# A two-block transformer on one core: chunks regrouped in the feed-forward, two norms' squares moved from GpSimd, operand steps made one block earlier

## The chip, the core and the metric

The kernel runs on one core of a Trainium2 chip. Five engines work there from queues of their own: TensorE (PE in the profile; PEld is its weight load), VectorE (DVE), ScalarE (ACT), GpSimd (POOL) and SyncE (SP, which only issues transfers here; POOL issues some too). An engine takes its instructions strictly in the order of its queue, and waits at the head of the queue for what the instruction needs. The metric is the time of one launch in device microseconds (us).

## The reference

Two transformer blocks on 512 tokens of 1024 features, in float32. The first has two layers; each mixes tokens (a short convolution in the first layer, attention in a window in the second, and attention to 256 memory rows in both) and ends in a feed-forward. The second block is sparse attention with retention beside it; its first norm follows directly on the first block's last norm. What the change touches is this, cut from the reference:

```
def rmsnorm(x, g):
    x32 = x.astype(jnp.float32)
    y = x32 * lax.rsqrt(jnp.mean(x32 * x32, axis=-1, keepdims=True) + EPS)
    return (y * g.astype(jnp.float32)).astype(x.dtype)
...
        x = x + jnp.concatenate([y_tok, y_mem], axis=-1) @ w_out
        h = rmsnorm(x, norm_ffn[i])
        x = x + (jax.nn.silu(h @ w_gate[i]) * (h @ w_up[i])) @ w_down[i]
    return rmsnorm(x, final_norm)
```

The feed-forward is 2816 wide.

## The kernel before, in words

The activations lie with features on the partitions: `self.x` is eight chunks of 128 features by 512 tokens. Every float32 product is made of three TensorE matmuls: each operand is split into a high part (ScalarE copies it, L70) and a low part (VectorE subtracts, L76 or L80), and high by high, low by high and high by low are added in PSUM (L120 to L122, or L575 to L577). Weights come through `weights`: a transfer on SP's queue into one of two raw buffers `wr`, then `wh` by ScalarE and `wl` by VectorE, three buffers each. A raw buffer is free for the next transfer when its last reader is done.

`ffn` runs over 22 chunks of 128 of the feed-forward's width, in the groups of `FFG`. Chunks 0 to 4 are plain (`plain_gate_up`: 48 matmuls of 512 columns). From chunk 5 on, gate and up together are seven smaller products (`gate_up`: 84 matmuls of 256 columns), with sums of weights (`pair_weights`: `s1` to `s4` by VectorE at L555, then split) and sums of activations. The latter, called B here, are made once a feed-forward by the generator `halves`, two chunks of x at a step, so four steps. While a group's chunks are computed, the down projection of the group before it is done between them: eight outputs `down`, one for each chunk of x, of 3 matmuls of 512 columns for each chunk in the group. VectorE subtracts each output from x (L638). `share` says how many of the eight come in which chunk. The last group's eight follow when all chunks are done; in the first layer's feed-forward the projections of the memory rows (`mem_kv`) stand ahead of them.

After the last group x is complete, and the next layer's norm needs the sum of its squares over features. `square_sum` adds the squares of the eight chunks to `acc` (after the second feed-forward also to `acc2`, weighted by a gain). With `first` false GpSimd squares chunks 0 to 6 (L157) and adds chunks 1 to 6 (L166); ScalarE squares chunk 7 (L159) and VectorE adds it. With `first` true ScalarE squares all eight and VectorE adds. `token_mean` sums `acc` over partitions with tiny matmuls (L174), `rsqrt` works on 4 columns, and `spread` makes from it a row over all partitions (L203, L206), called `Rb` in the second layer and `R` in the second block. The next projections use x without the norm's factor (`gained`: `gh` and `gl`, or `g`), and the factor is put on their results; they need `R` only when they are done.

The Python code is not the order in the queues: a scheduler in the compiler puts each engine's instructions into an order of its own, which is then fixed.

Of the kernel before, what the change touches and what calls it, by code (L numbers as in the profile page):

```python
# [21 lines left out]
NEG = -1.0e30  # L22
WMAX = 1152
KWORDS = 2 * 9 * 64
FFG = [(0, 4), (4, 8), (8, 12), (12, 16), (16, 19), (19, 22)]
PLAIN = 5


class Build:
# [590 lines left out]
    def ffn(self, layer, between_last=None):  # L620
        nc, T = self.nc, self.T
        gain = self.gain(2 + layer)
        h = self.gained(self.x, gain)
        R = B = act = None

        def down(i, act, g):

            f0, f1 = FFG[g]
            n = f1 - f0
            w = []  # L630

            def one(c):
                if not w:
                    w.extend(self.weights(T["w_down"][layer, i][:, f0 * 256:f1 * 256], 2 * n, 128))
                ps = self.psum("po" if (2 * i + c) % 3 == 2 else "tp")
                self.proj(ps, None, act, [t[:, c * n:c * n + n] for t in w])
                x = self.x[2 * i + c]
                nc.vector.tensor_tensor(x, x, ps, op=ALU.subtract)  # L638

            return [lambda: one(0), lambda: one(1)]  # L640

        for g, (f0, f1) in enumerate(FFG):
            last = act
            todo = [] if last is None else [p for i in range(4) for p in down(i, last, g - 1)]
            act = []
            n = f1 - f0
            shares = [0] * n if last is None else [4, 2, 1, 1] if f0 < PLAIN else [8 * (i + 1) // n - 8 * i // n for i in range(n)]
            for f, share in zip(range(f0, f1), shares):
                mine, todo = todo[:share], todo[share:]

                def between(i):
                    for p in mine[i * (len(mine) // 2):] if i else mine[:len(mine) // 2]:
                        p()

                if f < PLAIN:
                    a, R = self.plain_gate_up(layer, f, h, R)
                    if f == 0:
                        steps = self.halves(self.x, R, gain)
                    else:
                        sets = next(steps)  # L660
                    between(0)
                    between(1)
                else:
                    if f == PLAIN:
                        B = [[s[i] for s in sets] for i in range(7)]
                    a = self.gate_up(T["w_gu"][layer, f - PLAIN], B, between)
                act.append(a)
        if between_last:
            between_last()
        for i in range(4):  # L670
            for p in down(i, act, len(FFG) - 1):
                p()

    def layer_b(self):
        nc, T = self.nc, self.T
        hk = self.gained(self.x, self.gain(4), ["pa"] * 3 + ["pb"] * 5)
        rs, R = self.norm_row(1e-5, "Rb")
        rs = self.keep(rs, "rsb")
        h = self.gained(self.x, self.gain(1))
        xd = self.dr.tile([8, 128, 512], F32, name="xres")  # L680
        for c in range(8):
            nc.gpsimd.dma_start(xd[c], self.x[c])
        ks = []
        for b in range(2):
            ps = self.psum("pp")
            self.proj(ps, T["w_kv_k"][b], hk)
            kk = self.slot("t", name="k")
            self.mul(kk, ps, R)
            ks += self.stack_k(kk, tag="x")
        vs = []  # L690

        def done(tb, ps):
            v = self.value_tile()
            self.fill_values(v, ps, rs[:, tb:tb + 1])
            vs.append(v)
            if tb == 3:
                vs.append(self.last_value(ps, rs[:, 3:]))

        self.proj_tok(T["w_kv_v"], hk, 256, 4, done, tag=("pp", "lg"))
        mk, mv = self.mem1  # L700
        qs = []
        for b in range(2):
            qs += self.stack_q(self.queries(T["b_w_q"][6 + b], h, R))
        ym = self.mem_attention(qs, mk, mv)
        ys = []
        for pair in range(6):
            q = self.stack_q(self.queries(T["b_w_q"][pair], h, R))
            bias = self.bias(pair)
            po = self.psum("po")
            nc.tensor.matmul(po.rearrange("p (a b) -> p a b", a=4), self.zero, self.zero.unsqueeze(1).to_broadcast([128, 4, 128]), start=True, stop=False)  # L710
            for odd in range(2):
                self.band_head(po, 2 * pair + odd, odd, q[odd], ks, vs, bias[:, odd])
            ys.append(self.split(po, "b", name="y"))
        self.x = [self.slot("x", name="x") for _ in range(8)]
        for c in range(8):
            nc.sync.dma_start(self.x[c], xd[c])
        self.residual(T["b_w_out"], ys + ym, [6, 7, 0, 1, 2, 3, 4, 5])
# [209 lines left out]
    def second(self):  # L927
# [4 lines left out]
        g2 = self.const("g2", [128, 8])  # L932
        self.mul(g2, gf, gf)
        h = self.gained(self.x, gg)
        a1, a2 = self.square_sum(self.x, gain2=g2)
        m1 = self.token_mean(a1, 512, 1e-5, 1024.0)
        m2 = self.token_mean(a2, 512, 0.0, 1024.0)
        t = self.small(4, name="m3")
# [1 line left out]
        rs = self.keep(self.rsqrt(t), "rs12")  # L940
        R = self.spread(rs, "R2")
# [235 lines left out]
def _feat(w):  # L1177

    k, c = w.shape
    return np.ascontiguousarray(w.reshape(k // 128, 128, c // 128, 128).transpose(2, 1, 0, 3)).reshape(c // 128, 128, k)  # L1180
# [48 lines left out]
def _pack(i):  # L1229
# [18 lines left out]
    down = np.stack([_feat(m) for m in w["w_down"]]).reshape(2, 4, 2, 128, 22, 128).transpose(0, 1, 3, 2, 4, 5)  # L1248
    a["w_down"] = np.concatenate([down[:, :, :, :, f0:f1].reshape(2, 4, 128, -1) for f0, f1 in FFG], 3)
    a["w_kv_k"] = _feat(w["w_kv"][:, :256])  # L1250
# [46 lines left out]
```

## Time and profile before

| | before |
|---|---|
| median of 3 runs (lowest, highest) | 1681.77 us (1681.52, 1689.32) |
| profiled execution: time, span | 1686.65 us, 1684.9 us |
| mean granted TensorE clock | 0.987 of 2.4 GHz |
| PE busy | 1619.6 us, 96% |
| VectorE, ScalarE, GpSimd busy | 1248.2, 756.6, 196.4 us |

The span runs from the first to the last instruction; the launch's time is 1.75 us more. All times below are counted from the start of the span. In rows of the timeline, what stands in brackets is the idle time of the engine ahead of the instruction and what ended it.

### The profile page before, as it was taken

Reading aid. Unit: us, or ns where it says so; the run is one execution under the profiler, and the core shown is the slowest. Engines: PE = TensorE matmul, PEld = TensorE weight load, DVE = VectorE, ACT = ScalarE, POOL = GpSimd, SP = SyncE. Lnnn points to the kernel's source line nnn. Section 1 sums busy time; section 2 is a strip of 40 time slices with the busy share of each in tenths; the row PEclk is TensorE's granted clock in tenths of the full one; section 3 lists DMA queues with packets and bytes.
Section 4 is the critical chain, followed back from the end, with each engine's and each line's share of the span. In section 5 each row is a group of like instructions: output and inputs, shape, how many; then the busy total and the mean of one; then the engine's idle time right before and its main releaser. Section 6 shows DMA issues by size and latency. Waiting matters only on the chain.

```text
span 1684.9 us, 24388 instructions
## 1 busy us (share of the span) xinstructions
PE 1619.6 (96%) x9408; PEld 1415.5 (84%) x9408; DVE 1248.2 (74%) x2330; ACT 756.6 (45%) x1404; POOL 196.4 (12%) x186
## 2 busy tenths in 40 slices
PE   8999999999999699999999999979999999999997
PEld 6887888999999588888889999857788888888887
DVE  7866788787776869877877777579788977764443
ACT  6532244454445467634444444324556533333233
POOL 1112410000000600041000000151001000010010
PEclk9999999999999799999999999989999999999999
DMA  6222222332234522232233233332511122243342
GB/s 199 88 88 88 100 76 100 101 113 101 101 104 123 183 94 77 68 101 88 85 103 113 89 113 98 91 118 86 172 45 57 40 76 92 70 150 113 124 158 88
DMA packets 51572, 171.60 MB, mean 102 GB/s; under 512 B 6680, under 2 KB 6880, under 8 KB 51328
## 3 DMA queue, kind: packets, MB, share of 16 engines
q1 hardware_dynamic: 45504, 151.11, 27.1%
q0 software_dynamic: 5376, 18.82, 3.3%
q8 instruction: 74, 1.21, 0.3%
q14 instruction: 42, 0.34, 0.1%
q10 hardware_dynamic: 576, 0.11, 0.0%
HBM read 160.56 MB, written 11.81 MB: 102 GB/s over the span
## 4 chain that ended last, share of the span: by engine, by line
PE 71%; DVE 15%; DMA 7%; ACT 3%; issue 3%; POOL 1%; SPq 0%; DVEq 0%; ACTq 0%; POOLq 0%
PE pp L122 8%; PE pp L121 8%; PE pp L120 8%; PE lg L120 4%; PE lg L121 4%; PE lg L122 4%; DMA wr<-in_w_gu_dram 3%; DVE wl L80 3%; PE pp L575 3%; PE pp L576 2%; PE pp L577 2%; PE tp L262 2%; PE tp L120 2%; PE tp L121 2%; PE tp L122 2%
## 5 line engine op out<-in xcount | busy, mean ns | idle before, releaser
L70 ACT ACTIVATE wh<-wr 128x1024 fp32r<-128x1024 f32 (+3 forms) x246 | 251.9, 1025 | 371.7 <-PE pp L121 129.1
L80 DVE TENSOR_TENSOR wl<-wr,wh 128x1024 fp32r<-128x1024 f32 (+3 forms) x246 | 305.6, 1243 | 70.1 <-ACT wh L70 68.8
L122 PE MATMUL pp<-g,wl 128*128 128x512 f32 x592 | 235.0, 397 | 11.2 <-DVE wl L80 11.2
L120 PE MATMUL pp<-g,wh 128*128 128x512 f32 x592 | 235.8, 399 | 8.1 <-ACT wh L70 8.1
L121 PE MATMUL pp<-g,wh 128*128 128x512 f32 x592 | 234.1, 396 | 0.2 <-DVE g L76 0.2
L122 PEld LDWEIGHTS pp<-g,wl 128*128 128x128 f32 x592 | 112.2, 189 | 33.7 <-DVE wl L80 13.0
L120 PEld LDWEIGHTS pp<-g,wh 128*128 128x128 f32 x592 | 112.6, 190 | 30.3 <-ACT wh L70 8.9
L121 PEld LDWEIGHTS pp<-g,wh 128*128 128x128 f32 x592 | 112.4, 190 | 21.6 <-DVE g L76 0.9
L70 ACT ACTIVATE s<-s 128x512 fp32r<-128x512 f32 x136 | 85.0, 631 | 62.5 <-DVE s L555 59.7
L120 PE MATMUL tp<-acth,wh 128*128 128x512 f32 x264 | 104.4, 396 | 5.7 <-DVE x L638 3.3
L121 PE MATMUL tp<-actl,wh 128*128 128x512 f32 x264 | 104.0, 394 | 0.0
L122 PE MATMUL tp<-acth,wl 128*128 128x512 f32 x264 | 103.4, 392 | 0.0
L80 DVE TENSOR_TENSOR s<-s,s 128x512 fp32r<-128x512 f32 x136 | 90.3, 685 | 1.9 <-ACT s L70 1.7
L575 PE MATMUL pp<-Bh,s 128*128 128x256 f32 x272 | 77.5, 285 | 3.4 <-ACT g L70 3.4
L575 PE MATMUL lg<-Bh,s 128*128 128x256 f32 x272 | 77.8, 286 | 1.3 <-DVE u L582 1.3
L577 PE MATMUL pp<-Bh,s 128*128 128x256 f32 x272 | 77.4, 285 | 0.3
L577 PE MATMUL lg<-Bh,s 128*128 128x256 f32 x272 | 77.4, 285 | 0.0
L555 DVE TENSOR_TENSOR s<-wr,wr 128x512 f32<-128x512 f32 x68 | 46.8, 688 | 39.7 <-DMA wr<-in_w_gu_dram 39.7
L120 PEld LDWEIGHTS tp<-acth,wh 128*128 128x128 f32 x264 | 50.0, 190 | 16.4 <-ACT wh L70 2.6
L122 PEld LDWEIGHTS tp<-acth,wl 128*128 128x128 f32 x264 | 50.0, 190 | 10.6
L638 DVE TENSOR_TENSOR x<-x,tp 128x512 f32<-128x512 f32 x72 | 49.2, 683 | 12.6 <-PE tp L122 12.6
L576 PE MATMUL lg<-Bl,s 128*128 128x256 f32 x204 | 58.1, 285 | 0.0
(503 smaller groups left out, 4557.5 us busy)
## 6 DMA issues: line engine op xcount, KB each, us to landing
wr<-in_w_gu_dram SPq DMA_DIRECT2D x68, 512.0 KB, 3.8
wr<-in_w_in_dram SPq DMA_DIRECT2D x44, 512.0 KB, 3.5
wr<-in_w_down_dram SPq DMA_DIRECT2D x32, 512.0 KB, 3.7
wr<-in_a_w_in_dram SPq DMA_DIRECT2D x18, 512.0 KB, 3.5
wr<-in_w_down_dram SPq DMA_DIRECT2D x16, 384.0 KB, 3.3
wr<-in_w_gate_dram SPq DMA_DIRECT2D x10, 512.0 KB, 3.5
wr<-in_w_up_dram SPq DMA_DIRECT2D x10, 512.0 KB, 3.4
wr<-in_a_w_out_dram SPq DMA_DIRECT2D x8, 512.0 KB, 3.4
```

Of the source, the lines that this page charges most:

```text
L70: self.nc.scalar.activation(out, in_, AF.Copy, scale=scale)
L80: self.nc.vector.tensor_tensor(out, x, hi.bitcast(F32), op=ALU.subtract)
L120: mm(ps, ah, bh, start=start, stop=False)
L121: mm(ps, ah, bl, start=False, stop=False)
L122: mm(ps, al, bh, start=False, stop=stop)
L262: self.nc.tensor.transpose(ps[:, c:c + 128], src, self.ident)
L555: nc.vector.tensor_tensor(t, a, b, op=ALU.add)
L575: mm(ps, ah, bh, start=start and j == 0, stop=False, skip_group_check=not start)
L576: mm(ps, ah, bl, start=False, stop=False, skip_group_check=not start)
L577: mm(ps, al, bh, start=False, stop=j == 3, skip_group_check=not start)
L638: nc.vector.tensor_tensor(x, x, ps, op=ALU.subtract)
```

## The change

Three edits. The groups of chunks become 4, 4, 3, 4, 3, 4 in place of 4, 4, 4, 4, 3, 3, so the last down projection has four chunks and is 96 matmuls in place of 72; the total is the same, and the weights of `w_down` are packed to suit. The step of `halves` for x's first two chunks comes in chunk 0 instead of chunk 1, and so on: all four steps are done after chunk 3 instead of chunk 4. The two norms that follow a feed-forward (in `layer_b`, and at the start of `second`) take their squares from ScalarE and their sums from VectorE; the norm inside each layer, ahead of the feed-forward, stays as it was.

```
-FFG = [(0, 4), (4, 8), (8, 12), (12, 16), (16, 19), (19, 22)]
+FFG = [(0, 4), (4, 8), (8, 11), (11, 15), (15, 18), (18, 22)]
...
                     if f == 0:
                         steps = self.halves(self.x, R, gain)
-                    else:
-                        sets = next(steps)
+                    sets = next(steps, None) or sets
...
-        rs, R = self.norm_row(1e-5, "Rb")
+        rs, R = self.norm_row(1e-5, "Rb", True)
...
-        a1, a2 = self.square_sum(self.x, gain2=g2)
+        a1, a2 = self.square_sum(self.x, first=True, gain2=g2)
```

What this makes of the queues is seen at three places. The first is VectorE's queue at the end of the first feed-forward, from the last chunk of x (`x_88`) to the first split of a weight of the next layer (`wl_5583`, the first projection's). `acc` is the sum of squares, `m` and `ri` are the norm's small columns. Before:

```order
L638 TENSOR_TENSOR x_88<-x_88,tp_5445 128x512
L76 SCALAR_TENSOR_TENSOR g_5562<-x_86,gains,g_5562 128x512
L76 SCALAR_TENSOR_TENSOR g_5565<-x_87,gains,g_5565 128x512
L76 SCALAR_TENSOR_TENSOR gl_5485<-x_88,gains,gh_5484 128x512
L166 TENSOR_TENSOR acc_5488<-acc_5488,sq_5508 128x512
L76 SCALAR_TENSOR_TENSOR g_5568<-x_88,gains,g_5568 128x512
L176 TENSOR_SCALAR m_5516<-tp_5511 128x4
L80 TENSOR_TENSOR wl_5583<-wr_5581,wh_5582 128x1024
```

And now:

```order
L638 TENSOR_TENSOR x_88<-x_88,tp_5442 128x512
L166 TENSOR_TENSOR acc_5488<-acc_5488,sq_5505 128x512
L76 SCALAR_TENSOR_TENSOR g_5559<-x_85,gains,g_5559 128x512
L76 SCALAR_TENSOR_TENSOR gl_5485<-x_88,gains,gh_5484 128x512
L166 TENSOR_TENSOR acc_5488<-acc_5488,sq_5508 128x512
L76 SCALAR_TENSOR_TENSOR g_5562<-x_86,gains,g_5562 128x512
L176 TENSOR_SCALAR m_5516<-tp_5511 128x4
L76 SCALAR_TENSOR_TENSOR g_5565<-x_87,gains,g_5565 128x512
L183 TENSOR_SCALAR ri_5518<-m_5516 128x4
L76 SCALAR_TENSOR_TENSOR g_5568<-x_88,gains,g_5568 128x512
L184 TENSOR_SCALAR ri_5518<-ri_5518 128x4
L80 TENSOR_TENSOR wl_5583<-wr_5581,wh_5582 128x1024
```

Six more additions to `acc` stand in this queue ahead of the last (one is in the piece), and between `m` and the weight's split stand two more `g`. In TensorE's queue the place is the same before and after: four matmuls of the next layer, the tiny matmuls on `acc_5488`, then the first matmul that needs `wl_5583`.

The second place is TensorE's queue at the end of the second feed-forward, where the first projection of the second block (`pp_11094`) follows on the last down projection. Before, every row of the first matmuls up to the tiny ones on the two sums:

```order
L120 MATMUL pp_11094<-g_10954,wh_11096 128x512
L121 MATMUL pp_11094<-g_10954,wh_11096 128x512
L120 MATMUL pp_11134<-g_10954,wh_11136 128x512
L121 MATMUL pp_11134<-g_10954,wh_11136 128x512
L122 MATMUL pp_11094<-g_10954,wl_11097 128x512
...
L174 MATMUL tp_11010<-ones,acc_10978 128x2 x4
L174 MATMUL tp_11017<-ones,acc_2007_10979 128x2 x4
```

And now (eighteen matmuls of `pp_11094` are left out, in regular order):

```order
L120 MATMUL pp_11094<-g_10954,wh_11096 128x512
L121 MATMUL pp_11094<-g_10954,wh_11096 128x512
L122 MATMUL pp_11094<-g_10954,wl_11097 128x512
...
L174 MATMUL tp_11010<-ones,acc_10978 128x2 x4
L174 MATMUL tp_11017<-ones,acc_2007_10979 128x2 x4
L120 MATMUL pp_11094<-g_10975,wh_11096 128x512
```

The tiny matmuls, which wait for the sums, stood behind 13 matmuls and now stand behind 21. The split `wl_11097` stood in VectorE's queue behind the last chunk of x; it now stands behind the fourth:

```order
L638 TENSOR_TENSOR x_7098<-x_7098,tp_10868 128x512
L166 TENSOR_TENSOR acc_10978<-acc_10978,sq_10986 128x512
L80 TENSOR_TENSOR wl_11097<-wr_11095,wh_11096 128x1024
L638 TENSOR_TENSOR x_7099<-x_7099,tp_10888 128x512
L76 SCALAR_TENSOR_TENSOR g_10963<-x_7098,gg,g_10963 128x512
```

The third place is VectorE's queue in chunk 4, ahead of the first `gate_up` (chunk 5), whose raw weights are `wr_2264` and `wr_2265`. Before, the fourth step of `halves` (`Bh`, `t`) and three chunks of x stood between `u_2168` and the last reader of `wr_2264`, which is `s_461`:

```order
L80 TENSOR_TENSOR Bh_2190<-m_437_2177,Bh_2190 128x512
L638 TENSOR_TENSOR x_81<-x_81,tp_2202 128x512
L80 TENSOR_TENSOR Bh_2193<-t_438_2178,Bh_2193 128x512
L638 TENSOR_TENSOR x_82<-x_82,tp_2216 128x512
L80 TENSOR_TENSOR wl_2269<-wr_2264,wh_2268 128x1024
```

And now no step of `halves` stands there:

```order
L76 SCALAR_TENSOR_TENSOR u_2189<-lg_2158,Rf_345_1769 128x512
L80 TENSOR_TENSOR wl_2269<-wr_2264,wh_2268 128x1024
L80 TENSOR_TENSOR actl_2193<-u_2189,acth_2192 128x512
L80 TENSOR_TENSOR a_456_2272<-wr_2265,a_456_2272 128x512
L638 TENSOR_TENSOR x_81<-x_81,tp_2202 128x512
L555 TENSOR_TENSOR s_457_2275<-wr_2265,wr_2264 128x512
L555 TENSOR_TENSOR s_459_2280<-s_457_2275,wr_2264 128x512
L555 TENSOR_TENSOR s_461_2285<-wr_2264,wr_2265 128x512
```

The readers of `wr_2264` moved up; the fourth step's 11 instructions are one chunk earlier. Between the two feed-forwards, and behind the first projections of the second block, the queues of TensorE, VectorE and ScalarE are the same but for the order of some 40 rows of VectorE.

## Rows read from the trace of the kernel before

**Rows 1.** Busy us by stage: stretch, length, PE, PEld, DVE, ACT, POOL, PEclk, DMA share, GB/s.
```profile
262.00:350.00 88.00, 85.13 (x595) 78.83 (x594) 70.33 (x115) 41.95 (x70) 0.00 (x0) 1.00 0.31 102
815.00:895.00 80.00, 75.66 (x517) 70.14 (x516) 61.64 (x101) 36.25 (x61) 0.00 (x0) 0.98 0.30 94
350.00:500.00 150.00, 150.00 (x1028) 139.85 (x1027) 111.61 (x182) 68.81 (x113) 0.00 (x0) 1.00 0.31 103
560.00:592.00 32.00, 19.66 (x72) 15.29 (x71) 26.67 (x41) 11.07 (x16) 20.66 (x21) 0.73 0.49 166
1100.00:1137.00 37.00, 25.44 (x100) 19.77 (x100) 29.49 (x58) 9.48 (x12) 18.19 (x19) 0.82 0.32 111
```

**Rows 2.** Timeline of TensorE, end of the first feed-forward: start, duration, engine, line.
```profile
566.89 0.39 PE L120 MATMUL pp<-gh,wh 128*128 128x512 f32 x1
...
579.19 1.87 PE L174 MATMUL tp<-ones,acc 128*128 128x2 f32 x8 [10.94 <-DVE acc L166]
582.44 0.80 PE L122 MATMUL pp<-gh,wl 128*128 128x512 f32 x1 [1.38 <-DVE wl L80]
...
588.15 0.40 PE L120 MATMUL pp<-gh,wh 128*128 128x512 f32 x1
```

**Rows 3.** VectorE's groups by shape, 556 to 579: count, busy us, mean ns.
```profile
L76 DVE SCALAR_TENSOR_TENSOR g<-x,gains,g 128x512 fp32r<-128x512 f32 x7 | 9.6, 1385 | 0.0
L76 DVE SCALAR_TENSOR_TENSOR gl<-x,gains,gh 128x512 fp32r<-128x512 f32 x7 | 8.8, 1263 | 0.0
L638 DVE TENSOR_TENSOR x<-x,tp 128x512 f32<-128x512 f32 x5 | 3.4, 675 | 0.0
```

**Rows 4.** Busy us in two more stretches, columns as in the first group.
```profile
556.00:579.00 23.00, 12.24 (x53) 9.50 (x51) 22.92 (x23) 12.10 (x18) 22.08 (x21) 0.83 0.48 170
1150.00:1170.00 20.00, 17.63 (x116) 16.23 (x115) 19.60 (x36) 11.47 (x20) 1.66 (x1) 1.00 0.16 53
```

**Rows 5.** Timelines of VectorE, GpSimd and ScalarE, end of the first feed-forward.
```profile
571.24 2.91 DVE L76 SCALAR_TENSOR_TENSOR g<-x,gains,g 128x512 fp32r<-128x512 f32 x1
575.32 3.21 POOL L682 DMA_DIRECT2D xres<-x  x6
577.21 0.61 ACT L159 ACTIVATE sq<-x 128x512 f32<-128x512 f32 x1
577.80 0.74 DVE L76 SCALAR_TENSOR_TENSOR gl<-x,gains,gh 128x512 fp32r<-128x512 f32 x1
578.46 0.68 DVE L166 TENSOR_TENSOR acc<-acc,sq 128x512 f32<-128x512 f32 x1
```

**Rows 6.** Timeline of TensorE, end of the second feed-forward.
```profile
1096.18 0.39 PE L120 MATMUL po<-acth,wh 128*128 128x512 f32 x1
...
1098.22 0.39 PE L120 MATMUL tp<-acth,wh 128*128 128x512 f32 x1
...
1110.11 0.56 PE L120 MATMUL tp<-acth,wh 128*128 128x512 f32 x1 [2.16 <-DVE x L638]
...
1113.86 0.40 PE L120 MATMUL pp<-g,wh 128*128 128x512 f32 x1
...
1123.17 0.80 PE L122 MATMUL pp<-g,wl 128*128 128x512 f32 x1 [8.24 <-DVE wl L80]
...
1134.36 1.02 PE L206 MATMUL tp<-dg,ones 128*128 128x512 f32 x2
```

**Rows 7.** Timeline of VectorE: the first instruction that uses the row R.
```profile
1136.05 0.69 DVE L73 TENSOR_TENSOR f<-pp,R 128x512 f32<-128x512 f32 x1 [0.50 <-ACT R L70]
```

**Rows 8.** Timeline of TensorE: first matmuls of two blocks of gate_up in sequence.
```profile
296.42 0.28 PE L575 MATMUL pp<-B,wh 128*128 128x256 f32 x1
...
309.69 0.28 PE L575 MATMUL pp<-B,wh 128*128 128x256 f32 x1
```

**Rows 9.** Timeline of VectorE: the last reader of the first gate_up's first raw weights.
```profile
269.05 0.68 DVE L555 TENSOR_TENSOR s<-wr,wr 128x512 f32<-128x512 f32 x1
```

**Rows 10.** Timeline of TensorE: first matmul of the first layer's last down projection.
```profile
549.90 0.47 PE L120 MATMUL po<-acth,wh 128*128 128x512 f32 x1 [0.89 <-DVE s L336]
```

**Rows 11.** Timeline of ScalarE: the split of the first gate_up's first raw weights.
```profile
255.90 1.06 ACT L70 ACTIVATE wh<-wr 128x1024 fp32r<-128x1024 f32 x1 [1.84 <-DMA wr<-in_w_gu_dram]
```

## The prediction, written before the changed kernel had run

> **What bounds the kernel now.** I read the busy time by stage first, because a mean of 96% for TensorE says nothing of where the rest goes. In the middle of a feed-forward TensorE is busy 150.00 of 150.00 us: no change of order can gain there. It idles in four places [rows 1]: 32.00 − 19.66 = 12.34 us at the end of the first feed-forward, 37.00 − 25.44 = 11.56 at the end of the second, and 2.87 and 4.34 in their first `gate_up` blocks. All three edits aim at these, so the sum is made there.
>
> At the first end, the timeline of TensorE shows that it begins the next layer's matmuls at 566.89, does four, and then waits 10.94 for `acc` and 1.38 for a split weight; it resumes at 582.44 [rows 2]. Then it runs at the lower of its two clock levels (1.2 GHz): 13 matmuls take 5.71 us to 588.15, where at the full clock one output of nine takes 1098.22 − 1096.18 = 2.04 us, or 0.227 each [rows 2, 6]. That is 5.71 − 2.95 = 2.8 lost on top.
>
> Why is `acc` late? VectorE is busy 22.92 of the 23.00 us from 556 to 579, and GpSimd 22.08 [rows 4]. VectorE's 14 splits of x there take 1385 and 1263 ns, and one takes 2.91 us; the same split takes 0.74 at 577.80, where GpSimd computes nothing any more [rows 3, 5]. The update of x from PSUM takes its 675 ns throughout. So 14 splits cost 18.4 us instead of 10.4: 8 us of VectorE's queue go to GpSimd's squares and sums, and the last chunk of x, and `acc` behind it, are late by that.
>
> At the second end the same happens earlier: the down projection itself waits for x (11.56 − 8.24 = 3.32 in two waits), runs nine matmuls from 1110.11 to 1113.86 in 3.75 instead of 2.04, and then waits 8.24 for `wl` in VectorE's queue [rows 1, 6].
>
> **The change, part by part.**
>
> *First end.* The 13 instructions of arithmetic on GpSimd are gone; GpSimd only issues transfers. ScalarE gets seven more squares of 0.61, VectorE six more sums of 0.68 [rows 5]. ScalarE was busy 12.10 of 23.00, so 4.3 more fit [rows 4]. On VectorE a chunk of x is now one update, two splits and one sum, 0.68 + 2 × 0.74 + 0.68 = 2.84, some 0.08 less each in sequence, so 2.5; TensorE's output of 12 matmuls takes 2.72. VectorE keeps pace, where before it had 3.2 a chunk against 2.04. Behind the last update come a sum, two splits and the last sum: 0.7 + 0.6 + 0.7 + 0.7 + 0.7 = 3.4, so the wait of 10.94 becomes about 3 (TensorE has four matmuls to do meanwhile). From there to the weight it was 582.44 − 579.19 = 3.25; two splits more stand in that stretch of the queue, + 1.4. Gain: 7.9 − 1.4 = 6.5. The slow stretch behind it stays if the two waits, of 3 each, lower the clock as that of 2.16 did [rows 6]; otherwise 2.8 more.
>
> Ahead of it two things get tighter. The memory rows' projections have 1 output of nine instead of 2 as cover behind the last `gate_up`, 2.0 us less, and the first down matmul now uses the second pair's weights, whose load starts only when a raw buffer of the memory weights is free. TensorE already waits 0.89 at that spot [rows 10]. Bounds: nothing, or 2.0 plus one split by ScalarE of 1.06 [rows 11]. I take 1.5. A gain at the clock of between 0 and 2.8, say 1.5, evens this out. **First end: 6.5, from 3 to 10.**
>
> *Second end.* VectorE's chunk is one update, one split and two sums, again 2.5 to 2.9 against 2.72, so the two waits for x go (3.3 and 1.7 at the low clock). `wl_11097` stands five chunks earlier, so TensorE does not wait for it (8.24), and the tiny matmuls stand behind 21 matmuls, 4.8 us after the last down: the last sums end about 3.6 after it. No wait is left. Without waits TensorE reaches `pp` at 1113.86 − 3.3 − 1.7 = 1108.9; 21 matmuls (4.8), the tiny ones (at most the 1.87 of rows 2, twice as many at double the clock) and 23 matmuls (5.2) lead to L206 at 1120.8 instead of 1134.36 [rows 2, 6]. `f` follows 1.69 later as before, at 1122.4 instead of 1136.05 [rows 6, 7]. I count to `f` because VectorE sets the time after it (19.60 of 20.00 busy [rows 4]), so a lead of TensorE alone would be lost. **14, from 9 to 16**; the lower end is a wait of 5 for the sums, as if a chunk took VectorE 3.3.
>
> *Operand steps.* In chunk 4, the last reader of the first raw buffer ends at 269.73 [rows 9]. Its weights were split by ScalarE from 255.90 to 256.96 [rows 11]; from there the new queue has only a split of 1.2, one of `act`, `a`, x and three sums ahead of the release, 1.2 + 6 × 0.65 = 5.1, so it comes at about 262. The loads behind it start 4 to 8 us earlier, and the waits of the first blocks, 2.87 and 4.34, and 1.6 at the low clock, have that as cover. The steps cost nothing one chunk earlier: each chunk had one, now chunks 0 to 3 have it. **6.5 of 8.8, from 0 to 9.**
>
> *Groups.* Blocks with two outputs of nine matmuls are shorter than any steady one before: 84 × 0.12 + 2 × 2.04 = 14.2 us, eight in each feed-forward. The supply has followed at 309.69 − 296.42 = 13.27 [rows 8], but over two blocks only. Bounds 0 and 16 × 0.5; I take **−1**.
>
> Two rules of the Trainium skill bear on this. Rows 3 and 5 show that splits with two inputs in SBUF stretch and updates with one input in PSUM don't. "SBUF — State Buffer", section "Who interferes with whom", says that a VectorE instruction with two SBUF inputs contends with GpSimd instructions that read SBUF, and that the loser blocks for the whole instruction; the trace's 2.91 for one of 0.74, 2.2 more than alone, needs two GpSimd instructions in its way, not one. By the rule the sums that VectorE takes over have GpSimd no more as a rival, and the total stands. "ScalarE: Activation LUTs", section "What ACT_TABLE_LOAD costs", speaks against the squares: a change of table set costs 2.66 us, and if each square among the copies cost one, 16 would be 43 us. The square at 577.21 stands among copies at 0.61 without one [rows 5]; the sum goes by that.
>
> **Sum.** 6.5 + 14 + 6.5 − 1 = 26. The profiled execution took 1686.65, 4.9 more than the median of 1681.77; its waits are taken as the median's, so 1686.65 − 26 = 1660.7 in its terms and **1655.8** in those of the median.
>
> **Rivals.**
>
> *A: only the ends gain.* The first blocks wait on transfers, whose time doesn't change, and the freed VectorE time is spent waiting for them: operand steps 0. For it: VectorE is busy only 70.33 of 88.00 there [rows 1], so it isn't full. Against: the raw buffer's release at 269.73 is VectorE's. 1681.8 − 19.5 = 1662.3.
>
> *B: the stretched splits are not GpSimd's doing* but the transfers' (170 GB/s in that stretch [rows 4]). Then the splits stay at 1.3, VectorE's chunk is 4.0 us against 2.72, and each end is later by the six or so sums of 0.68: − 4 at each, with + 5.5 left of the rest: 1684. Against: at 577.80, between GpSimd's six issues and with transfers under way, a split took 0.74 [rows 5]. The same skill page ("SBUF: two separate sides") says that engines and transfers don't contend; by it this rival is out.
>
> *C: slower.* The 16 blocks of 14.2 us outrun the supply of weights. If a block's three loads and their splits need more than 14.2 + 26/16 = 15.8 us, the loss eats the gain; at 17, it is 45 − 27 = 18 us: 1700. Against: 13.27 [rows 8], and 15.6 us blocks without any wait [rows 1].
>
> *D: nothing moves*, because what is gained at the ends is waited for behind them, where VectorE is full: 1681. Against: VectorE's queue itself starts 13.7 earlier.
>
> **Chances.** Forecast 0.62, A 0.22, a larger gain (all of the bounds, 1681.8 − 36 = 1646) 0.07, B and D 0.06, C 0.03. The range that leaves out no more than 2 in 10 is 1646 to 1667. What a measurement here can tell from no change is 0.5%, 8.4 us: faster 0.91, same 0.05, slower 0.04.
>
> **What would show it.** Right: at the first end TensorE waits about 3 us for `acc`; every split of x takes 0.75; at the second end no wait over 1 us until `R` is used, and the granted clock stays at 1.00 there; waits under 3 us in all in the first blocks; no new waits in blocks with two outputs. Wrong: splits over 1 us without GpSimd's arithmetic (B), TensorE waiting for `wh` or `g` in chunks 11 to 14 and 18 to 21 (C), or a new wait before the first layer's last down projection of more than 3 us.

## The result, and the profile after

The changed kernel takes 1664.85 us (median of 4 runs, 1661.98 to 1666.17) against 1683.68 for the kernel before in the same runs: a ratio of 0.9884, 95% interval 0.9866 to 0.9903. That is 19.5 us faster. The prediction said 26 us and 1655.8, with a range of 1646 to 1667. The spans of the two profiled executions differ by 1684.9 − 1663.6 = 21.3 us.

The view of busy time by stage of the changed kernel, the stages as in [rows 1] with the second end where it now lies (stretch, length, PE, PEld, DVE, ACT, POOL, PEclk, DMA share, GB/s):

```profile
262.00:350.00 88.00, 85.46 (x583) 79.44 (x583) 64.13 (x104) 38.94 (x66) 0.00 (x0) 0.98 0.34 108
815.00:895.00 80.00, 77.14 (x530) 71.91 (x529) 60.40 (x98) 37.57 (x62) 0.00 (x0) 0.98 0.32 105
560.00:592.00 32.00, 26.53 (x105) 21.27 (x104) 26.40 (x52) 18.16 (x28) 4.85 (x8) 0.84 0.51 177
1080.00:1120.00 40.00, 39.52 (x181) 32.31 (x180) 36.91 (x78) 17.89 (x24) 6.59 (x11) 1.00 0.48 162
```

At the second end TensorE idles 0.48 of 40 us and its clock stays at 1.00; at the first end its idle time went from 12.34 to 5.47. The first blocks, which the operand steps were to clear, idle 2.54 and 2.86 us: in the first feed-forward that is what it was (2.87).

The timeline of TensorE in the changed kernel shows the same places as [rows 2, 6, 10] (start, duration, operation; in brackets the idle time ahead and what ended it):

```profile
265.21 0.28 PE L575 MATMUL pp<-B,wh 128*128 128x256 f32 x1
...
273.26 0.44 PE L575 MATMUL pp<-Bh,s 128*128 128x256 f32 x1 [2.14 <-ACT g L70]
...
528.34 0.40 PE L120 MATMUL tp<-acth,wh 128*128 128x512 f32 x1
...
541.12 0.39 PE L142 MATMUL tp<-wh,gm 128*128 128x256 f32 x1 [2.32 <-ACT wh L70]
547.23 0.50 PE L120 MATMUL po<-acth,wh 128*128 128x512 f32 x1 [0.85 <-ACT wh L70]
...
574.37 1.86 PE L174 MATMUL tp<-ones,acc 128*128 128x2 f32 x8 [2.62 <-DVE acc L166]
579.08 0.79 PE L122 MATMUL pp<-gh,wl 128*128 128x512 f32 x1 [2.85 <-DVE wl L80]
...
1078.01 0.40 PE L120 MATMUL tp<-acth,wh 128*128 128x512 f32 x1
...
1106.61 1.84 PE L174 MATMUL tp<-ones,acc 128*128 128x2 f32 x16
...
1113.65 1.02 PE L206 MATMUL tp<-dg,ones 128*128 128x512 f32 x2
```

The wait of 10.94 for `acc` is 2.62 and that of 1.38 for the weight is 2.85 (the prediction had 3 and 2.8). At the second end the tiny matmuls and L206 wait for nothing. That was close: VectorE's last sum there,

```profile
1105.67 0.68 DVE L166 TENSOR_TENSOR acc<-acc,sq 128x512 f32<-128x512 f32 x1
```

ends 0.26 us before TensorE comes to it at 1106.61. New are the waits at 273.26 and 541.12 and, at the same spot of the second feed-forward,

```profile
823.30 0.58 PE L575 MATMUL pp<-Bh,s 128*128 128x256 f32 x1 [2.24 <-ACT g L70]
```

The granted clock falls at two of them. Busy time by stage of the changed kernel, right behind 273.26 and 823.30:

```profile
273.40:276.80 3.40, 3.40 (x15) 3.20 (x16) 2.97 (x6) 1.67 (x4) 0.00 (x0) 0.51 0.20 24
823.00:826.40 3.40, 3.10 (x13) 3.06 (x14) 3.11 (x6) 1.53 (x4) 0.00 (x0) 0.50 0.00 0
```

Each of these stretches at the lower level (1.2 GHz) costs some 1.7 us, half its length, against the upper one. Before, the first feed-forward's blocks ran at 1.00 throughout (0.98 now in the first stage above), and the second's had one such stretch behind the wait of 1.74 at 884.13.

With these rows the 21.3 us can be placed. The change also moves matmuls from one stretch to the next (behind the last `gate_up` there is one output of nine instead of two, and the last down has 96 matmuls instead of 72), and each is 0.227 us of TensorE. So the first layer's blocks lose 15 matmuls, its memory rows lose 9 and its last down gains 24. In the second layer the last down is counted with the outputs that stand behind the last `gate_up`. The gain of a stretch is its time before, plus the work moved in, minus its time after.

| stretch of TensorE | before | work moved in | after | gain | predicted |
|---|---|---|---|---|---|
| first layer: first `gate_up` to end of the last | 265.80 | −3.4 | 263.13 | −0.7 | +2.75 |
| memory rows, to the last down | 18.34 | −2.0 | 18.89 | −2.6 | −1.5 |
| last down to the second layer's first `gate_up` | 268.90 | +5.4 | 267.92 | +6.4 | 6.5 + 1.5 |
| second layer: first `gate_up` to end of the last | 269.20 | −3.4 | 262.86 | +2.9 | +2.75 |
| last down to L206 | 46.36 | +3.4 | 35.64 | +14.1 | 14 |
| all the rest | 816.30 | 0 | 815.16 | +1.1 | 0 |

(The prediction has 6.5 − 1 for steps and groups in both feed-forwards together; 2.75 is half of it. Of the 8.8 us of waits that it names, 2.87 lie in the first.) The two ends came out near their working; most of what is missing lies in the first feed-forward's blocks and the memory rows. A row sets one execution against one: the kernel below in which GpSimd works on old tiles has the changed kernel's order on the other engines and takes 261.02 us in place of 263.13 in the first row, with a wait of 1.89 in place of 2.14 and the granted clock at 1.00 behind it. So 2 us in a row can be chance.

### The profile page after: what moved, and what is told of

It reads as the page before. It is cut to its first block, busy times and chain, and to the rows that moved or that the text cites. A ratio compares the mean times of both kernels' runs of the same rounds, so it can differ in the third digit from the quotient of the medians.

```text
span 1663.6 us, 24425 instructions
## 1 busy us (share of the span) xinstructions
PE 1617.0 (97%) x9408; PEld 1415.1 (85%) x9408; DVE 1238.1 (74%) x2342; ACT 763.1 (46%) x1418; POOL 162.7 (10%) x160
## 4 chain that ended last, share of the span: by engine, by line
PE 75%; DVE 12%; DMA 5%; issue 3%; ACT 3%; POOL 1%; SPq 0%; DVEq 0%; ACTq 0%; POOLq 0%
PE pp L122 8%; PE pp L120 8%; PE pp L121 8%; PE lg L120 4%; PE lg L121 4%; PE lg L122 4%; PE pp L575 3%; DMA wr<-in_w_gu_dram 3%; PE pp L576 3%; PE pp L577 3%; PE tp L120 3%; DVE wl L80 3%; PE tp L121 3%; PE tp L122 3%; PE tp L262 2%
## 5 line engine op out<-in xcount | busy, mean ns | idle before, releaser
L596 ACT ACTIVATE g<-g 128x512 f32<-128x512 f32 x34 | 21.5, 632 | 83.3 <-DVE g L582 83.3
L575 PEld LDWEIGHTS pp<-Bh,s 128*128 128x128 f32 x272 | 53.0, 195 | 6.8 <-ACT g L70 6.6
L576 PE MATMUL pp<-Bl,s 128*128 128x256 f32 x204 | 58.5, 287 | 0.0
```

What stands on the lines that cost most here:

```text
L575: mm(ps, ah, bh, start=start and j == 0, stop=False, skip_group_check=not start)
L576: mm(ps, ah, bl, start=False, stop=False, skip_group_check=not start)
L596: nc.scalar.activation(g, g, AF.Silu)
```

## The experiments

Each kernel was timed in five rounds beside the kernel before on the same chip, and is compared by its ratio to it. The ratio of the changed kernel is 0.9884, from the runs of the result above; 0.001 is 1.7 us. Theory 1 was: GpSimd's arithmetic stretches VectorE's splits; at an end TensorE waits for whatever stands late in VectorE's queue; so the norms and the groups gain together what neither gains alone, and the operand steps only move a wait in the first feed-forward.

### One edit alone

```diff
-        rs, R = self.norm_row(1e-5, "Rb")
+        rs, R = self.norm_row(1e-5, "Rb", True)
...
-        a1, a2 = self.square_sum(self.x, gain2=g2)
+        a1, a2 = self.square_sum(self.x, first=True, gain2=g2)
```

> The kernel before with the squares by ScalarE and the sums by VectorE in the two norms, groups and operand steps as before. Theory 1 (two edits work together): every split of x falls to 0.75 us, but an output of the last down projection is 2.04 us of TensorE against 2.5 to 2.9 of VectorE, and the split of the first weight stands in VectorE's queue behind all ten sums and splits that follow the last chunk of x, so at the second end the wait for that weight stays, at 5 to 8 us in place of 8.24, while the waits for x (3.3) go; gain 6 at each end, 1670 us in all. Rival (the norms carry nearly all of it): the second end gains its whole 16 us and the first its 7, 1659 us.

Measured: 1676.47 us, ratio 0.9925 (0.9911 to 0.994), 12.6 us faster: theory 1's 12 in all and not the rival's 23, though the parts differ. VectorE's groups by shape at the first end (count, busy us, mean ns):

```profile
L76 DVE SCALAR_TENSOR_TENSOR gl<-x,gains,gh 128x512 fp32r<-128x512 f32 x8 | 6.0, 749 | 1.5 <-ACT gh L70 1.5
L76 DVE SCALAR_TENSOR_TENSOR g<-x,gains,g 128x512 fp32r<-128x512 f32 x8 | 5.9, 747 | 0.0
```

Every split is short, as in the changed kernel. At the second end TensorE still waits, for the sums rather than for the weight, as its timeline shows:

```profile
1113.58 3.57 PE L174 MATMUL tp<-ones,acc 128*128 128x2 f32 x16 [6.29 <-DVE acc L166]
```

From the last down to L206 it takes 36.89 us; before 46.36. So the norms alone gain 9.5 of the 14.1 there (expected was 6), and 3.3 of 6.4 at the first end (expected was 6).

```diff
-FFG = [(0, 4), (4, 8), (8, 12), (12, 16), (16, 19), (19, 22)]
+FFG = [(0, 4), (4, 8), (8, 11), (11, 15), (15, 18), (18, 22)]
```

> The kernel before with the new groups alone. Theory 1: splits of x stay at 1.2 to 1.4 us; the split of the first weight of the second block stands five chunks earlier in the queue, so its wait of 8.24 goes and a shorter one for the sums comes, gain 8 to 10 at the second end; at the first end 2 to 5, and 3 lost ahead of it at the memory rows; 1671 us. The 14.2 us blocks with two outputs wait for nothing. Rival (regrouping is a cost that the norms have to pay back): 1684 us.

Measured: 1692.26 us, ratio 1.0027 (1.0014 to 1.004): 4.5 us slower. Theory 1 failed here by its number, and the rival's sign held. VectorE's groups at the first end, and four rows of TensorE's timeline:

```profile
L76 DVE SCALAR_TENSOR_TENSOR gl<-x,gains,gh 128x512 fp32r<-128x512 f32 x8 | 9.9, 1237 | 1.7 <-ACT gh L70 1.7
L76 DVE SCALAR_TENSOR_TENSOR g<-x,gains,g 128x512 fp32r<-128x512 f32 x8 | 9.2, 1149 | 0.0
```

```profile
370.26 0.39 PE L575 MATMUL pp<-Bh,s 128*128 128x256 f32 x1 [1.61 <-ACT g L70]
...
928.59 0.39 PE L575 MATMUL pp<-Bh,s 128*128 128x256 f32 x1 [3.51 <-ACT g L70]
...
1127.45 0.80 PE L121 MATMUL pp<-g,wh 128*128 128x512 f32 x1 [2.89 <-DVE g L76]
1131.11 3.58 PE L174 MATMUL tp<-ones,acc 128*128 128x2 f32 x16 [2.86 <-DVE acc L166]
```

The weight's split does come early, and its wait of 8.24 [rows 6] is gone, but the splits of x that it overtook are now late instead: from the last down to L206 the kernel takes 49.82 us for 3.4 us more work than in 46.36, a gain of nothing. VectorE is full there, and another order of the same work moves the wait. And the blocks with two outputs of nine do wait for weights (1.61 and 3.51 at the first of them): by the same account as in the table the blocks lose 3.4 and 2.4 us.

```diff
-                    else:
-                        sets = next(steps)
+                    sets = next(steps, None) or sets
```

> The kernel before with the operand steps one block earlier alone. Theory 1: the raw buffer comes free near 262 us in place of 269.73, but ScalarE's queue then has the next chunk's splits, which wait for their transfer, ahead of the copy that empties a PSUM bank, and TensorE waits some 2 us there near 273 and again near 823; net gain 0 to 2 us, 1681 us. Rival (the earlier release is worth what the prediction gave it, and what is lost comes from the groups): 1675 us.

Measured: 1684.58 us, ratio 0.9985 (0.9972 to 0.9998), 2.5 us faster: nearer to theory 1. By the spans' accounts the first feed-forward's blocks lose 0.7 and the second's gain 3.8, as they do in the changed kernel (−0.7 and +2.9). TensorE's waits are 2.18 at 274.43 and 2.24 at 826.79. The three edits alone add up to 12.6 − 4.5 + 2.5 = 10.6 us, and together they give 19.5: the rest comes only when they stand together.

### GpSimd busy again

The first try added a tile to the constants to write to, and narrowed the weight tiles to make room.

```diff
+            if gp and c < last:
+                for i in range(4):
+                    nc.gpsimd.tensor_tensor(self.gp, x[:, 240 * (i % 2):240 * (i % 2) + 240], x[:, 240 * (i % 2):240 * (i % 2) + 240], op=ALU.mult)
```

> The changed kernel, in which GpSimd also multiplies parts of x by themselves at the two ends (28 instructions of 240 columns each end, four for each of x's chunks 0 to 6) into a tile that nobody reads; the queues of the other four engines are the same row for row. Theory 1 (GpSimd's reads stretch VectorE's splits): the splits of x take 1.1 to 1.4 us again, x from PSUM stays at 0.68, the first end's wait for the sums grows from 2.6 to some 8 us, 1675 us or more. Rival (the transfers stretched them): splits stay at 0.75 and the time at 1665.

Measured: 1690.35 us, ratio 1.0019 (1.0009 to 1.003), 23 us slower than the changed kernel by the ratios. But it was also slower where GpSimd had nothing extra to do, and all matmuls of 512 columns followed each other more slowly, so two causes were mixed. The next two kernels separate them: one with the tiles alone,

```diff
-WMAX = 1152
+WMAX = 1120
...
+        self.gp = self.const("gp", [128, 240])
```

> The changed kernel with a tile of 240 columns that nobody uses among the constants and with the weight tiles 1120 columns wide in place of 1152, as the kernel with GpSimd's extra work had it; the queues of all engines are the same row for row as the changed kernel's, only addresses in SBUF differ. In that earlier run one matmul of 512 columns took 0.232 us on the way to the next, everywhere, also far from GpSimd's extra work, where the changed kernel takes 0.228. Theory 2 (addresses, not GpSimd, slowed the matmuls): 0.232 here too, and with some 4000 to 5000 such matmuls 15 to 18 us more, 1681 us. Rival (GpSimd's work or that run's chip did it): 0.228 and 1665 us.

Measured: 1673.81 us, ratio 0.9919 (0.9905 to 0.9932), 5.9 us slower than the changed kernel. The mean spacing of 512-column matmuls is 0.232 us here and 0.228 in the changed kernel, so the addresses do it and neither GpSimd nor the chip (the next kernel ran on the same one, at 0.228); but the price is a third of what was expected. Part of the rest is that waits got shorter: at the second feed-forward's first block with `gate_up` it is 1.38 in place of 2.24, and the granted clock stays at 1.00 behind it. The other writes into an old tile and leaves all addresses as they are:

```diff
+            if gp and c < last:
+                for i in range(4):
+                    h = slice(256 * (i % 2), 256 * (i % 2) + 256)
+                    nc.gpsimd.tensor_tensor(self.mR, x[:, h], x[:, h], op=ALU.mult)
```

> The changed kernel, in which GpSimd multiplies halves of x's chunks 0 to 6 by themselves at the two ends (28 instructions of 256 columns each end) and writes them into the row of the memory norm, which nobody reads any more; no tile is added, and the queues of the other engines are the same row for row. Theory 1 (GpSimd's reads stretch VectorE's splits): splits of x take 1.1 to 1.4 us at the ends, x from PSUM 0.68, the wait for the sums at the first end some 7 us in place of 2.6 and one of 5 at the second; matmuls keep their 0.228; 10 to 12 us more, 1675 to 1677. Rival (transfers stretched the splits, and the addresses alone made the earlier run slow): 1665, splits at 0.75.

Measured: 1682.02 us, ratio 0.9967 (0.9955 to 0.9979), 14 us slower than the changed kernel, with spacing 0.228. VectorE's groups by shape at the first end in the changed kernel:

```profile
L76 DVE SCALAR_TENSOR_TENSOR gl<-x,gains,gh 128x512 fp32r<-128x512 f32 x8 | 6.0, 748 | 0.8 <-ACT gh L70 0.8
L166 DVE TENSOR_TENSOR acc<-acc,sq 128x512 f32<-128x512 f32 x7 | 4.8, 687 | 0.0
L76 DVE SCALAR_TENSOR_TENSOR g<-x,gains,g 128x512 fp32r<-128x512 f32 x6 | 4.5, 748 | 0.4 <-ACT g L70 0.4
L638 DVE TENSOR_TENSOR x<-x,tp 128x512 f32<-128x512 f32 x6 | 4.1, 683 | 2.2 <-PE tp L122 2.2
```

and with GpSimd busy, VectorE's own queue being the same row for row (L170 and L642 are L166 and L638):

```profile
L76 DVE SCALAR_TENSOR_TENSOR gl<-x,gains,gh 128x512 fp32r<-128x512 f32 x8 | 8.6, 1071 | 0.8 <-ACT gh L70 0.8
L76 DVE SCALAR_TENSOR_TENSOR g<-x,gains,g 128x512 fp32r<-128x512 f32 x7 | 7.4, 1057 | 0.0
L170 DVE TENSOR_TENSOR acc<-acc,sq 128x512 f32<-128x512 f32 x7 | 6.4, 917 | 0.0
L642 DVE TENSOR_TENSOR x<-x,tp 128x512 f32<-128x512 f32 x6 | 4.1, 677 | 2.2 <-PE tp L122 2.2
```

The groups with two inputs in SBUF are stretched (748 to 1071, 687 to 917); the update from PSUM is not (683 and 677). TensorE's wait for the sums grows from 2.62 to 7.59 at the first end and from nothing to 6.38 at the second. That is theory 1, and rival B of the prediction is out: the transfers are the same. GpSimd reads and writes here, and which of the two stretches VectorE was not parted.

### One edit undone

```diff
-                    sets = next(steps, None) or sets
+                    else:
+                        sets = next(steps)
```

> The changed kernel with the operand steps back in chunks 1 to 4. Theory 1 (the steps gave 2 to 5 us, nearly all of it in the second feed-forward): first blocks as before, waits of about 1.2 near 274 and 827 and of 1.7 at the low clock near 882; 1667 to 1670. Rival (they gave nothing, since the wait for a PSUM bank took what the raw buffer gave): 1665.

Measured: 1671.09 us, ratio 0.9899 (0.9885 to 0.9912), 2.6 us slower by the ratios, whose intervals overlap, and 1670.5 − 1663.6 = 6.9 by the profiled spans. So the side is theory 1's, but the time alone doesn't show it. By the stretches of the table the blocks take 2.0 and 6.3 us longer. Norms and groups, alone 12.6 − 4.5 = 8.1 us, give 17.0 here: those two gain together what neither gains alone. In the timelines of ScalarE and TensorE at the first block with two outputs in the second layer, the wait of the groups alone is back:

```profile
919.27 0.63 ACT L70 ACTIVATE a<-wr 128x512 fp32r<-128x512 f32 x1 [2.98 <-DMA wr<-in_w_gu_dram]
920.06 0.63 ACT L70 ACTIVATE s<-s 128x512 fp32r<-128x512 f32 x1 [0.17 <-DVE s L555]
920.60 0.36 ACT L70 ACTIVATE g<-pp 128x256 f32<-128x256 f32 x1
```

```profile
921.02 0.39 PE L575 MATMUL pp<-Bh,s 128*128 128x256 f32 x1 [3.39 <-ACT g L70]
```

ScalarE waits 2.98 for a weight transfer; behind it in its queue stands the copy that empties the PSUM bank that TensorE needs. In the changed kernel no wait over 0.3 stands at that block. So the earlier steps remove this wait; that they do it by giving the supply a lead, which the shorter blocks then use up, is an inference.

```diff
-FFG = [(0, 4), (4, 8), (8, 11), (11, 15), (15, 18), (18, 22)]
+FFG = [(0, 4), (4, 8), (8, 12), (12, 16), (16, 19), (19, 22)]
```

> The changed kernel with the old groups. Theory 1 (the groups cost by themselves, 4 to 5 us as measured alone, but pay once the splits are short, since an output of 2.72 us then gives VectorE time and the first weight's split comes early): 4 to 5 us slower than the changed kernel, ratio to before 0.991, with a wait of some 6 us for the sums at the second end. Rival (the costs add up): without the groups 5 us faster than the changed kernel, ratio 0.985.

Measured: 1669.51 us, ratio 0.9897 (0.9882 to 0.9912): slower by 0.0013, 2.2 us, with 6.29 of waiting for the sums at the second end. The side is theory 1's and not the rival's, at half the size, and the intervals overlap. The groups cost 4.5 us alone and cost nothing, or gain a little, beside the other two edits; from the last down to L206 this kernel takes 36.83 us, so the groups take 36.83 + 3.4 − 35.64 = 4.6 off there.

### What else could go

```diff
-FFG = [(0, 4), (4, 8), (8, 11), (11, 15), (15, 18), (18, 22)]
+FFG = [(0, 4), (4, 8), (8, 11), (11, 14), (14, 18), (18, 22)]
```

> The changed kernel with groups of 4, 4, 3, 3, 4, 4: the last two groups have four chunks each, so the outputs that stand behind the last gate_up ahead of the memory rows are of 12 matmuls in place of 9. If the 4.6 us of waits from 500 to 560 come from too short a cover there, 1 to 2 us of them go and the time is 1663; if they come from the raw buffer of the memory weights alone, they stay and it is 1665.

Measured: 1668.35 us, ratio 0.9884 (0.987 to 0.9898), the same as the changed kernel. The wait at the memory rows for their weights goes from 2.32 to 1.90 only, and the last down then starts with one of 2.29. More matmuls as cover do not remove it. It comes with the regrouping: the kernel with the old groups and the other two edits has no such wait, and its memory rows take 18.31 us, as before.

```diff
-        h = self.gained(self.x, self.gain(1))
         xd = self.dr.tile([8, 128, 512], F32, name="xres")
...
             self.proj(ps, T["w_kv_k"][b], hk)
+            if b == 0:
+                h = self.gained(self.x, self.gain(1))
             kk = self.slot("t", name="k")
```

> The changed kernel, in which the splits of x for the queries (g) are called behind the first projection of the keys in the second layer. VectorE's queue then has that projection's weight split three chunks of x before the end in place of behind all of them, and TensorE's tiny matmuls stand behind 16 of its matmuls in place of 4, as they did at the second end. Theory 1 (at an end TensorE waits for what stands late in VectorE's queue, and the order decides it): the waits of 2.6 and 2.85 at the first end shrink to under 1.5 together, and the granted clock stays up; 4 to 6 us faster than the changed kernel, ratio 0.985. Rival (VectorE has to do the same work before the norm's row is there, and TensorE waits for that row a little later): within 1 us of the changed kernel, 0.988.

Measured: 1660.06 us, ratio 0.9836 (0.9821 to 0.985), 8 us faster than the changed kernel by the ratios and 5.0 by the spans. It is the fastest kernel of this study, and its interval lies apart from the changed kernel's. Stage 560 to 592 in the windows, and TensorE's wait for the sums:

```profile
560.00:592.00 32.00, 28.72 (x134) 23.43 (x133) 26.23 (x51) 18.61 (x29) 4.87 (x8) 0.95 0.54 181
```

```profile
576.76 1.05 PE L174 MATMUL tp<-ones,acc 128*128 128x2 f32 x8 [2.77 <-DVE acc L166]
```

The weight's wait of 2.85 is gone and the clock of the stage is 0.95 in place of 0.84. The wait for the sums stayed, 2.77, against the "under 1.5 together" that was expected: VectorE now does the weight's split ahead of the sums and ends them later, so the rival had a part of it.

```diff
-        self.copy(g1, U)
+        nc.vector.tensor_copy(g1, U)
...
-        self.copy(g2, U)
+        nc.vector.tensor_copy(g2, U)
...
-        self.copy(u, U)
+        nc.vector.tensor_copy(u, U)
```

> The changed kernel, in which VectorE and not ScalarE copies the three results out of PSUM in each gate_up block. If the waits of 2.14 and 2.24 in the first blocks come from copies that stand on ScalarE behind the split of weights whose transfer is not there yet, they fall to about 1, since on VectorE the second copy stands behind the first of these splits but ahead of the others; some 2 us faster, ratio 0.987. Rival (the block waits for the weights themselves): the waits stay, now put down to VectorE, and the time is that of the changed kernel or, with 0.42 us more for VectorE per copy, above it.

Measured: 1668.31 us, ratio 0.989 (0.9875 to 0.9905), no different from the changed kernel. The waits of the first blocks shrank from 2.14 to 1.42 and from 2.24 to 1.86, now put down to VectorE, and new ones of 0.4 to 1.0 stand in later blocks. Where the copy stands accounts for part of the wait; that the rest is the transfers themselves was not shown.

The last kernel has both of these diffs.

> Both of the last two edits. If each removes its own waits, their gains add: 6 to 8 us faster than the changed kernel, ratio 0.984. If VectorE is too full for both, no better than the better one of them alone.

Measured: 1666.54 us, ratio 0.9885 (0.9869 to 0.9902). The gains don't add; it is 8 us behind the kernel with the operands later alone by the ratios, and 4.5 by the spans. By the spans 1.9 of 4.5 are lost between the norm ahead of the second feed-forward and the sums at its end, and 2.6 behind that. Why was not followed further.

## Why the prediction was right, and where it was off

The forecast lay 9 us below the time, within its range; the mechanism it gives for the ends held, and the term for the operand steps did not.

**The ends.** Both came out near their working: 6.4 of the 6.5 + 1.5 in that stretch, and 14.1 of 14. At the first, the waits fell by 8.3 for the sums and grew by 1.5 for the weight, as worked out (7.9 and 1.4); new waits of 0.53 and 0.49 at the start of the last down took 0.9 back. At the second the margin was thinner than worked out: the sums end 4.5 us after the last down, not 3.6, and the tiny matmuls come at 4.8, so that there is no wait at all is in part luck. (The weight's split stands four chunks earlier in VectorE's queue, not five.) Its reading of [rows 3, 5], that GpSimd's instructions stretch VectorE's splits, was made certain by the kernel that only gives GpSimd work: same queues on the other four engines, splits at 1071, 14 us. The rule of the Trainium skill ("SBUF — State Buffer", section "Who interferes with whom"), by which VectorE instructions with two SBUF inputs contend with GpSimd's, agrees with what was stretched there and what was not. The prediction gave its 14 to the norms and the queue's order together and did not part them: by the runs alone, the norms bring 9.5 there and the groups nothing, and the whole change 14.1.

**The clock behind the first end.** Of the 1.5 us that the prediction set aside for it 0.6 came: the granted clock in that stage is 0.84, up from 0.73 [rows 1], and from the end of the weight's wait to L206 it is 5.85 us now and 6.41 before. The clock rose to 0.95 in the two kernels that removed one of the two waits.

**The squares on ScalarE** took 616 ns each among its copies, and the profile has two table loads (L612), as before, so the rule that the prediction weighed against the change does not bear on these instructions.

**Operand steps: the step that was off.** The prediction took 6.5 us for them. The release of the raw buffer came where it was put: SP's row for the load behind it is now

```profile
262.03 0.33 SPq L111 DMA_DIRECT2D wr<-in_w_down_dram  x1
```

The prediction said 262. What it left out is that the order of ScalarE's queue changes with the edit. Before, the second copy of `g` out of PSUM stood ahead of the next weights' splits:

```profile
270.90 0.37 ACT L70 ACTIVATE g<-pp 128x256 f32<-128x256 f32 x1
273.37 1.06 ACT L70 ACTIVATE wh<-wr 128x1024 fp32r<-128x1024 f32 x1 [2.10 <-DMA wr<-in_w_down_dram]
```

Now two splits stand ahead of it. That the compiler puts them there because it expects the weights sooner is an inference. ScalarE's timeline in the changed kernel:

```profile
269.75 1.06 ACT L70 ACTIVATE wh<-wr 128x1024 fp32r<-128x1024 f32 x1 [2.26 <-DMA wr<-in_w_gu_dram]
272.31 0.63 ACT L70 ACTIVATE a<-wr 128x512 fp32r<-128x512 f32 x1 [1.50 <-DMA wr<-in_w_gu_dram]
272.84 0.37 ACT L70 ACTIVATE g<-pp 128x256 f32<-128x256 f32 x1
```

ScalarE waits for two transfers, 2.26 and 1.50, and only then empties the bank; TensorE waits 2.14 at 273.26 for it, and the clock that falls behind this wait takes 1.7 more. The sign "waits under 3 us in all in the first blocks" holds for each feed-forward by itself (2.54 and 2.86) and not for both together. The term was read on VectorE and on SP; on ScalarE it was not. Rival A came nearer in time (1662.3 against 1664.85) and has half the cause: the blocks do wait on transfers, but the steps are worth 2.5 us alone and, though not clear of noise, about as much in the changed kernel. That A's sum of 19.5 is the measured gain to the digit is chance.

**Groups.** The −1 was too small for the blocks: alone the groups lose 5.8 us in the blocks, rival C's mechanism at a smaller size, which the earlier steps then largely remove. So the terms for steps and groups, 5.5 together, measured 2.2 in the two stretches of blocks, and they can't be parted, since each changes the other's worth.

**Memory rows.** −1.5 was predicted, within 0 and −3.06; it is −2.6. The new wait is the 2.32 at 541.12, for the memory rows' own weights; ScalarE's row ahead of it is

```profile
540.01 1.06 ACT L70 ACTIVATE wh<-wr 128x1024 fp32r<-128x1024 f32 x1 [2.50 <-DMA wr<-in_w_mem_v_dram]
```

The first down weights, which the prediction had named, hold TensorE for 0.85; before, it waited 0.89 there for VectorE [rows 10]. Why the memory rows' weights land so late was not followed.

**The sum.** The upper bounds of the parts add up to 35, not 36, so that the lower end of its range would be 1647.

## What to carry to other kernels

When an edit makes a resource come free earlier, follow every queue whose order changes, the one that empties PSUM above all: an in-order engine that stands at a load holds everything behind it. When VectorE is full at a joint, moving one split ahead only moves the wait; take work or stretch off it first, and then the order is worth something. A test load on an engine should leave every tile where it was, or be run beside a kernel that moves the tiles alone.

## What was not expected of the hardware

Moving tiles in SBUF changed TensorE's rate. In the changed kernel, as in the kernel before, the tiles of operands and split weights start at multiples of 256 bytes by the compiled program; with the shifted tiles, at 64 or 192 bytes beyond one. From the row of the memory norm to the norm ahead of the first feed-forward TensorE has no wait over 0.6 us. In the changed kernel that stretch is

```profile
55.12 1.22 PE L206 MATMUL tp<-dg,ones 128*128 128x256 f32 x2 [2.46 <-DVE dg L203]
...
203.08 0.95 PE L174 MATMUL tp<-ones,acc 128*128 128x2 f32 x8
```

and with the shifted tiles

```profile
57.20 0.70 PE L207 MATMUL tp<-dg,ones 128*128 128x256 f32 x2 [2.25 <-DVE dg L204]
...
207.82 0.95 PE L175 MATMUL tp<-ones,acc 128*128 128x2 f32 x8
```

that is 147.96 and 150.62 us for the same queue, at a granted clock of 0.99 in both. The spacing of 512-column matmuls rose from 0.228 to 0.232; that of 256-column ones in dense blocks did not (0.120 and 0.119). Which of the moved tiles does it was not tried.
